# Order of the three-term products: high part of the weights for all k first, then the low part

## Chip, cores and metric

One core of a Trainium2 chip runs the whole program in one launch. The metric is the device time in microseconds (us), as the median of several runs. Before the change it is 2635.63 us (three runs, 2633.51 to 2636.17).

## The reference, cut to what matters

Two token groups, 128 context tokens and 512 latent tokens, pass through two layers with the same weights. Each layer is feed-forward, mixer, feed-forward, each with a modulated norm ahead of it and a gated residual behind it:

```
hn = modulate(rms_norm(x, norm_g[i, 0]), m[:, 0], m[:, 1])
x  = x + 0.5 * m[:, 2] * swiglu(hn, w_gate, w_up, w_down)     # 1024 -> 2816 -> 1024
hn = modulate(rms_norm(x, norm_g[i, 1]), m[:, 3], m[:, 4])
x  = x + m[:, 5] * mix(hn)        # layer 0: SSD scan + pooling; layer 1: gMLP + convolution
hn = modulate(rms_norm(x, norm_g[i, 2]), m[:, 6], m[:, 7])
x  = x + 0.5 * m[:, 8] * swiglu(hn, ...)
```

`swiglu(h) = (silu(h @ w_gate) * (h @ w_up)) @ w_down`. Everything is float32.

## The kernel before

**Tiling.** Activations lie transposed: channels on the 128 partitions, all 640 tokens in the free dimension, cut into two halves A and B of 320. A product with 1024 input channels is a sum over k = 0..7 of 128x128 weight blocks against 128x320 activations; the down projections of the feed-forward sum over the 5 or 6 hidden blocks of a group.

**Three terms.** To keep float32 accuracy with the fast F32R matmul, weights and activations are each split into a high part (a cast) and a low part (source minus high): ScalarE writes `wh`, then VectorE writes `wl` (`w_split`, L219 and L220); activations likewise (`split`, L376 and L377; `apply_mod`, L385 and L387). A block is then three matmuls in one PSUM bank, high x high, high x low, low x high (`mm3`, L392, L393, L394). The weights of one output block, for all k, are a *unit*: one `wh` and one `wl` tile, so each is written by one instruction, 128x1024 for eight blocks and 128x768 for six.

**Units.** `run_units` (L396) makes input projections, a unit at a time, k by k; with `kouter` it goes over k outside and over the units inside. In layer 0's mixer the first unit of half B is `dt`, 32 columns wide (L1016). `out_mms` (L425) makes output projections, through `out_task` (L430, one half) or `out_add` (L438, both halves, where `late=1` holds the last k back in the first block). The pooling branch of that mixer (`pool_mm`, L906) has an output projection of four k. The last output projection of a feed-forward or mixer goes through `out_phase` with `last`: its tasks come in the order A0 A1 A2 A3 B0 A4 B1 A5 B2 A6 B3 A7 B4 B5 B6 B7, so that a unit stays in use over three more A tasks. After B4 stands the matmul of the next norm's sum (`finish`, L368), and the next stage begins in `boundary` with half A, k outside, while half B is still being normed.

**Buffers.** All `wh` and `wl` tiles share a ring of nine buffers (`WB`, L30), four and a half units; raw weights have four (`RB`). A `wl` that finds no free buffer waits until TensorE has read the tile that lies there for the last time.

**Feed-forward.** Gate and up of most hidden blocks are made in `products` (L748) with seven instead of eight products per pair of halves (P1 to P7, sums of weights and of activations); a product is four k blocks x three terms = twelve matmuls (L761 to L764). A PSUM bank takes several products in turn, and ScalarE copies it out in between (`tap`, L745), so the next product in a bank waits for the tap. Each of the four feed-forwards has four groups of hidden blocks; a group's products are followed by its down projection.

**Order.** TensorE's order is the program's own. The order of ScalarE, VectorE, GpSimd and SyncE is set when the program is built, by a planner that goes by program order, by when operands are ready in its own timing, and by offsets such as `TAP_EARLY`; each engine then runs its list in that order. Semaphores make an instruction wait for its operands and buffers.

Of the kernel before, what the change touches and what calls it, by code (L numbers as in the profile page):

```python
# [20 lines left out]
TH = 320  # L21
# [38 lines left out]
A, B = 0, 1  # L60
SL = (slice(0, TH), slice(TH, T))
# [12 lines left out]
def build(tc, ap):  # L74
    nc = tc.nc
    V, S, TE, G = nc.vector, nc.scalar, nc.tensor, nc.gpsimd
    ctx = ExitStack()
    with ctx:
# [12 lines left out]
        def nm(p):  # L91
            uid[0] += 1
            return f"{p}_{uid[0]}"
# [35 lines left out]
        def open_phase(bufs):  # L129
            state["ctx"] = ExitStack()  # L130
            state["pool"] = state["ctx"].enter_context(tc.tile_pool(name=nm("phase"), bufs=bufs, reuse_waits="tile"))
# [11 lines left out]
        def psum(cols=512):  # L143
            return pspool.tile([P, cols], F32, tag="ps", name=nm("ps"))
# [17 lines left out]
        units = {}  # L162
# [106 lines left out]
        def W(key):  # L269
            i, left = index[key], LOOK  # L270
            prefetch(i)
            while i + 1 < len(plan) and left > 0:
                i += 1
                left -= 2 if plan[i][0] == "s" else 1
                if wpos[0] <= i and plan[i][0] == "s" and not state.get("sums"):
                    break
                prefetch(i)
            return loaded[key]
# [3 lines left out]
        def open_mod():  # L282
            crow[:] = [state["pool"].tile([P, D], F32, tag=f"crow{i}", name=nm("crow"), bufs=1) for i in range(2)]
            junk[:] = [state["pool"].tile([P, D], mybir.dt.bfloat16, tag="junk", name=nm("junk"), bufs=1)]
            for i, t in enumerate(crow):
                if kept:
                    nc.scalar.dma_start(out=t, in_=kept[0][i].partition_broadcast(P))
                else:
                    nc.scalar.dma_start(out=t, in_=ap["cc"][i].partition_broadcast(P))
                    S.activation(out=t, in_=t, func=AF.Silu)  # L290
            if not kept:
                kept.append(dpool.tile([2, D], F32, name="silu_rows"))
                for i, t in enumerate(crow):
                    nc.scalar.dma_start(out=kept[0][i:i + 1], in_=t[0:1, :])
            mod_load()
# [79 lines left out]
        def split(src, hi, lo):  # L375
            S.copy(hi, src)  # L376
            V.tensor_sub(lo, src, hi)  # L377
# [13 lines left out]
        def mm3(ps, wh, wl, xh, xl, start, stop):  # L391
            TE.matmul(ps, lhsT=wh, rhs=xh, start=start, stop=False)  # L392
            TE.matmul(ps, lhsT=wh, rhs=xl, start=False, stop=False)  # L393
            TE.matmul(ps, lhsT=wl, rhs=xh, start=False, stop=stop)  # L394

        def run_units(H, keys, hn, kouter=False, mid=None):  # L396
            pss = []
            ws = []
            for key in keys:
                ws.append(W(key))  # L400
                pss.append(psum())

            def one(i, k):
                wh, wl = ws[i]
                m = units[keys[i]][2]
                mm3(pss[i][:m, :TH], wh[k], wl[k], hn.hi(k, H), hn.lo(k, H), k == 0, k == 7)
            if kouter:
                for k in range(8):
                    for i in range(len(keys)):
                        one(i, k)  # L410
                    if mid and k in mid:
                        mid[k]()
            else:
                for i in range(len(keys)):
                    for k in range(8):
                        one(i, k)
            return pss

        def x_update(H, m, ps, L, gidx):
# [3 lines left out]
                                       in1=x[m][:, a:b], op0=ALU.mult, op1=ALU.add)  # L423

        def out_mms(H, ps, w, sh, sl, ks, n):  # L425
            wh, wl = w
            for k in ks:
                mm3(ps[:, :TH], wh[k], wl[k], sh[k][:, SL[H]], sl[k][:, SL[H]], k == 0, k == n - 1)

        def out_task(H, m, key, sh, sl, L, gidx, last):  # L430
            n = len(sh)
# [238 lines left out]
        def ffn(L, f, prev):  # L670
            isc, ish, ig = (1, 0, 2) if f == 0 else (7, 6, 8)
            head = HEAD.get((L, f), NSTD)
            keys = [[("g", L, f, j), ("u", L, f, j)] for j in range(head)]
# [3 lines left out]
            def h_tile(j):  # L677
                hts[j] = state["pool"].tile([P, 2, T], F32R, tag="h", name=nm("h"), bufs=6)

            def post(H, j, pg, pu):  # L680
                if j not in hts:
                    h_tile(j)
                sg = tmp()
                state["silu"] = S.activation(out=sg, in_=pg[:, :TH], func=AF.Silu).ins
                V.tensor_mul(sg, sg, pu[:, :TH])
                split(sg, hts[j][:, 0, SL[H]], hts[j][:, 1, SL[H]])

            if prev is None:
                hn, pss = startup(keys[0] + keys[1][:1])
                open_phase(1)  # L690
                open_mod()
                for H in (A, B):
                    post(H, 0, pss[H][0], pss[H][1])
                for H in (A, B):
                    pu, = run_units(H, keys[1][1:], hn)
                    post(H, 1, pss[H][2], pu)
            else:
                hn, pa = boundary(keys[0] + keys[1], L, isc, ish, prev, Quads)
                open_phase(1)
                post(A, 0, pa[0], pa[1])  # L700
                post(A, 1, pa[2], pa[3])
                for j in range(2):
                    pb = run_units(B, keys[j], hn)
                    post(B, j, pb[0], pb[1])
                with tc.issue_after(state["silu"]):
                    open_mod()
# [36 lines left out]
            def tap(src):  # L743
                t = tmp()
                S.copy(t, src[:, :TH])  # L745
                return t

            def products(js, lead=()):  # L748
                bank, got, ended = {}, {}, set()
                for j, p in product_order(js, lead):  # L750
                    if p == "P1":
                        W(("s", L, f, j))
                    wh, wl = loaded["s", L, f, j][p]
                    xh, xl = X[p]
                    b = "a" if p in CHAIN[0] else "c" if p in CHAIN[1] else "b"
                    if (j, b) not in bank:
                        bank[j, b] = psum()
                    ps = bank[j, b]
                    first = p in ("P1", "P5", "P2")
                    final = p in ("P4", "P3", "P2")  # L760
                    for k in range(4):  # L761
                        for n, (l, r) in enumerate(((wh, xh), (wh, xl), (wl, xh))):
                            TE.matmul(ps[:, :TH], lhsT=l[k], rhs=r[:, k, :], start=(first and k == 0 and n == 0),  # L763
                                      stop=(k == 3 and n == 2), skip_group_check=True)  # L764
                    with tc.high_priority(offset=TAP_EARLY):
                        if p in ("P1", "P6", "P7", "P5"):
                            got[j, p] = tap(ps)
                        if p == "P2":
                            V.tensor_add(got[j, "P1"], ps[:, :TH], got[j, "P1"])
                            S.activation(out=got[j, "P1"], in_=got[j, "P1"], func=AF.Silu)  # L770
                        if p == "P3":
                            V.tensor_add(got[j, "P6"], ps[:, :TH], got[j, "P6"])
                            S.activation(out=got[j, "P6"], in_=got[j, "P6"], func=AF.Silu)
                        if (p == "P7" and (j, "P5") in got) or (p == "P5" and (j, "P7") in got):
                            V.tensor_add(got[j, "P7"], got[j, "P7"], got[j, "P5"])
                        ended.add((j, p))
                        if p in ("P4", "P3") and (j, "P4") in ended and (j, "P3") in ended:
                            hf = ph.tile([P, T], F32, tag="hf", name=nm("hf"), bufs=2)
                            V.scalar_tensor_tensor(out=hf[:, SL[A]], in0=bank[j, "a"][:, :TH], scalar=-1.0, in1=got[j, "P1"],
                                                   op0=ALU.mult, op1=ALU.mult)  # L780
                            V.scalar_tensor_tensor(out=hf[:, SL[B]], in0=got[j, "P7"], scalar=-1.0,
                                                   in1=got[j, "P6"], op0=ALU.mult, op1=ALU.mult)
                            h_tile(j)
                            split(hf, hts[j][:, 0, :], hts[j][:, 1, :])
                    if p == "P1":
                        pump(rate_j)
# [793 lines left out]
```

## Time and profile before

| what | value |
|---|---|
| median of the runs | 2635.63 us |
| profiled execution: its own time, its span | 2630.1 us, 2628.3 us |
| granted TensorE clock, mean over the span | 0.991 |
| TensorE matmul | 2520.9 us busy, 96%, 17241 instructions |
| VectorE | 1932.4 us busy, 74% |
| ScalarE | 1226.9 us busy, 47% |
| chain that ended last | 36% TensorE in the shares by engine |

Busy TensorE time counts a matmul until its modelled end, so matmuls that follow each other overlap in the rows: a 128x320 matmul is shown with 0.31 us, and the next starts 0.147 us after it. What TensorE loses shows as a longer step from one start to the next.

### The profile page before, as it was taken

How to read it: one execution, taken by the hardware profiler on the slowest of the kernel's cores; microseconds unless marked ns; L12 is line 12 of the kernel's file. 1: busy time of each engine (PE TensorE's matmuls, PEld its weight loads, DVE VectorE, ACT ScalarE, POOL GpSimd, SP SyncE). 2: the span in 40 equal slices, each digit the busy share in tenths (PEclk: the TensorE clock that was granted, in tenths of full speed). 3: DMA queues.
4: the chain of work that ended last, by engine and by line, in shares of the span. 5: the costliest groups of instructions: out<-in, count | busy, mean ns of one | idle time of the engine just before them, and what ended most of it. 6: DMA issues, size and time to landing. Idle time of an engine off the chain costs nothing. (4 is left out here: it accounts for less than half of the span.)

```text
span 2628.3 us, 43699 instructions
## 1 busy us (share of the span) xinstructions
PE 2520.9 (96%) x17241; PEld 2431.4 (93%) x17241; DVE 1932.4 (74%) x3259; ACT 1226.9 (47%) x2299; POOL 153.6 (6%) x254
## 2 busy tenths in 40 slices
PE   7999999999999999999999999999999999999997
PEld 5999989899989999999899999989879999999997
DVE  6878878689986977777687778766885749554465
ACT  4443535458763535445454444433223525444552
POOL 0011010000000010110001011000000000101100
PEclk9999999999999999999999999999999999999999
DMA  7487785122122476776337687634432124656641
GB/s 285 135 214 211 209 223 170 58 71 66 55 62 78 119 212 176 214 211 164 109 103 218 182 219 222 167 101 128 130 107 71 51 73 132 176 134 154 155 120 59
DMA packets 139650, 377.31 MB, mean 144 GB/s; under 512 B 17458, under 2 KB 24114, under 8 KB 138932
## 3 DMA queue, kind: packets, MB, share of 16 engines
q1 hardware_dynamic: 111280, 296.06, 34.4%
q0 software_dynamic: 24624, 70.79, 15.4%
q10 hardware_dynamic: 3540, 7.66, 0.9%
q8 instruction: 135, 2.21, 0.3%
q14 instruction: 71, 0.58, 0.1%
HBM read 328.39 MB, written 3.68 MB: 126 GB/s over the span
## 5 line engine op out<-in xcount | busy, mean ns | idle before, releaser
L220 DVE TENSOR_TENSOR wl<-wr,wh 128x1024 fp32r<-128x1024 f32 (+3 forms) x393 | 390.9, 998 | 282.0 <-ACT wh L219 109.2
L219 ACT CAST wh<-wr 128x1024 fp32r<-128x1024 f32 (+3 forms) x393 | 339.7, 869 | 398.7 <-DMA wr<-in_wd 134.9
L394 PE MATMUL ps<-h,wl 128*128 128x320 f32 x1408 | 437.9, 311 | 9.8 <-DVE wl L220 9.8
L392 PE MATMUL ps<-h,wh 128*128 128x320 f32 x1408 | 437.6, 311 | 4.3 <-ACT h L376 4.3
L393 PE MATMUL ps<-h,wh 128*128 128x320 f32 x1408 | 437.1, 310 | 1.5 <-DVE h L377 1.5
L763 PE MATMUL ps<-quad,wh 128*128 128x320 f32 x1800 | 400.4, 310 | 5.4 <-ACT tmp L745 5.0
L763 PE MATMUL ps<-th,wh 128*128 128x320 f32 x1200 | 377.0, 314 | 26.0 <-ACT tmp L745 21.5
L763 PE MATMUL ps<-th,wl 128*128 128x320 f32 x1200 | 374.8, 312 | 3.2 <-DVE wl L220 3.2
L763 PE MATMUL ps<-tl,wh 128*128 128x320 f32 x1200 | 374.4, 312 | 0.0
L323 DVE CUSTOM_DVE_ANT_0 junk<-wm,crow,cv 128x1024 bf16<-128x1024 f32 x256 | 327.7, 1280 | 3.0
L392 PE MATMUL ps<-pair,wh 128*128 128x320 f32 (+1 forms) x976 | 308.9, 317 | 5.7 <-ACT pair L385 1.5
L763 PEld LDWEIGHTS ps<-quad,wh 128*128 128x128 f32 x1800 | 302.3, 189 | 6.5 <-ACT tmp L745 5.8
L393 PE MATMUL ps<-pair,wh 128*128 128x320 f32 (+1 forms) x976 | 304.1, 312 | 1.6 <-DVE pair L387 1.4
L394 PE MATMUL ps<-pair,wl 128*128 128x320 f32 (+1 forms) x976 | 303.3, 311 | 0.0
L763 PE MATMUL ps<-quad,wl 128*128 128x320 f32 x900 | 279.2, 310 | 0.7 <-DVE wl L220 0.7
L394 PEld LDWEIGHTS ps<-h,wl 128*128 128x128 f32 x1408 | 265.2, 188 | 14.0 <-DVE wl L220 14.0
L392 PEld LDWEIGHTS ps<-h,wh 128*128 128x128 f32 x1408 | 265.4, 188 | 5.4 <-ACT h L376 5.1
L393 PEld LDWEIGHTS ps<-h,wh 128*128 128x128 f32 x1408 | 265.3, 188 | 3.1 <-DVE h L377 2.4
L763 PEld LDWEIGHTS ps<-th,wh 128*128 128x128 f32 x1200 | 228.1, 190 | 32.1 <-ACT tmp L745 26.8
L220 DVE TENSOR_TENSOR wl<-ws,wh 128x1024 fp32r<-128x1024 f32 x150 | 182.9, 1221 | 97.6 <-ACT wh L219 42.2
L763 PEld LDWEIGHTS ps<-th,wl 128*128 128x128 f32 x1200 | 228.3, 190 | 4.6 <-DVE wl L220 4.5
L763 PEld LDWEIGHTS ps<-tl,wh 128*128 128x128 f32 x1200 | 228.4, 190 | 0.0
(261 smaller groups left out, 4416.4 us busy)
## 6 DMA issues: line engine op xcount, KB each, us to landing
wm<-in_wm SPq DMA_DIRECT2D x128, 512.0 KB, 4.4
wr<-in_wgu SPq DMA_DIRECT2D x75, 512.0 KB, 4.4
ws<-in_wgu SPq DMA_DIRECT2D x150, 256.0 KB, 4.0
ws<-in_wgu POOLq DMA_DIRECT2D x75, 512.0 KB, 5.7
x<-y POOLq DMA_DIRECT2D x96, 320.0 KB, 5.6
wr<-in_wd SPq DMA_DIRECT2D x64, 384.0 KB, 3.5
wr<-in_wd SPq DMA_DIRECT2D x64, 320.0 KB, 3.6
wr<-in_wgu SPq DMA_DIRECT2D x75, 256.0 KB, 3.5
```

The source lines that it names most:

```text
L219: S.copy(hi, src)
L220: state["paced"] = V.tensor_sub(lo, src, hi).ins
L323: V.tensor_tensor_reduce(out=junk[0], in0=w, in1=crow[cond], scale=1.0, scalar=cvc("b_mod", L * 72 + idx * KC + c), op0=ALU.mult, op1=ALU.add,
L392: TE.matmul(ps, lhsT=wh, rhs=xh, start=start, stop=False)
L393: TE.matmul(ps, lhsT=wh, rhs=xl, start=False, stop=False)
L394: TE.matmul(ps, lhsT=wl, rhs=xh, start=False, stop=stop)
L763: TE.matmul(ps[:, :TH], lhsT=l[k], rhs=r[:, k, :], start=(first and k == 0 and n == 0), stop=(k == 3 and n == 2), skip_group_check=True)
```

## The change

A helper `mm_high_first` issues, for the given k, high x high and high x low of each k, and only then low x high of each k. `out_mms` always uses it. `run_units` uses it where k is inside, except for the first `paced` units of a call; only the call for half B after a feed-forward's boundary passes 1 there (for its first pair of units), and all others leave it at 0. The `kouter` path keeps `mm3`. In `products` the loops over k and over the three terms change places: four high x high, four high x low, four low x high. The matmuls are the same in number and shape.

```diff
+        def mm_high_first(ps, w, xh, xl, ks, n):
+            wh, wl = w
+            for k in ks:
+                TE.matmul(ps, lhsT=wh[k], rhs=xh[k], start=(k == 0), stop=False)
+                TE.matmul(ps, lhsT=wh[k], rhs=xl[k], start=False, stop=False)
+            for k in ks:
+                TE.matmul(ps, lhsT=wl[k], rhs=xh[k], start=False, stop=(k == n - 1))
+
-        def run_units(H, keys, hn, kouter=False, mid=None):
+        def run_units(H, keys, hn, kouter=False, mid=None, paced=0):
...
                 for i in range(len(keys)):
-                    for k in range(8):
-                        one(i, k)
+                    if i < paced:
+                        for k in range(8):
+                            one(i, k)
+                    else:
+                        mm_high_first(pss[i][:units[keys[i]][2], :TH], ws[i], [hn.hi(k, H) for k in range(8)],
+                                      [hn.lo(k, H) for k in range(8)], range(8), 8)
...
         def out_mms(H, ps, w, sh, sl, ks, n):
-            wh, wl = w
-            for k in ks:
-                mm3(ps[:, :TH], wh[k], wl[k], sh[k][:, SL[H]], sl[k][:, SL[H]], k == 0, k == n - 1)
+            mm_high_first(ps[:, :TH], w, [t[:, SL[H]] for t in sh], [t[:, SL[H]] for t in sl], ks, n)
...
-                    pb = run_units(B, keys[j], hn)
+                    pb = run_units(B, keys[j], hn, paced=1 - j)
...
-                    for k in range(4):
-                        for n, (l, r) in enumerate(((wh, xh), (wh, xl), (wl, xh))):
+                    for n, (l, r) in enumerate(((wh, xh), (wh, xl), (wl, xh))):
+                        for k in range(4):
                             TE.matmul(ps[:, :TH], lhsT=l[k], rhs=r[:, k, :], start=(first and k == 0 and n == 0),
                                       stop=(k == 3 and n == 2), skip_group_check=True)
```

## Rows read from the trace of the kernel before

**Rows 1.** Part 1 of the page: busy us (share of span) x instructions, by engine.
```profile
PE 2520.9 (96%) x17241; PEld 2431.4 (93%) x17241; DVE 1932.4 (74%) x3259; ACT 1226.9 (47%) x2299; POOL 153.6 (6%) x254
```

**Rows 2.** TensorE's waits, whole span: waiter, releaser, total us, times, longest us.
```profile
PE ps L763 <- ACT tmp L745: 26.5, 23, 4.0
PE ps L394 <- DVE wl L220: 16.8, 24, 0.9
...
PE ps L763 <- DVE wl L220: 3.9, 6, 0.7
```

**Rows 3.** Timeline of TensorE in the startup: start, us, instruction; first and last of 21.
```profile
36.83 0.60 PE L604 MATMUL ps<-quad,wl 128*128 128x320 f32 x3
...
39.91 0.60 PE L604 MATMUL ps<-quad,wh 128*128 128x320 f32 x3
```

**Rows 4.** Timeline of TensorE within products; first and last of 36 matmuls.
```profile
1000.10 0.31 PE L763 MATMUL ps<-th,wh 128*128 128x320 f32 x1
...
1005.23 0.31 PE L763 MATMUL ps<-th,wl 128*128 128x320 f32 x1
```

**Rows 5.** Timeline of TensorE, last down projection (six k), start of task A7.
```profile
1755.78 0.31 PE L393 MATMUL ps<-h,wh 128*128 128x320 f32 x1
1756.70 0.41 PE L394 MATMUL ps<-h,wl 128*128 128x320 f32 x1 [0.61 <-DVE wl L220]
```

**Rows 6.** Timeline of VectorE, same place; in brackets the idle time before.
```profile
1754.45 0.49 DVE L364 TENSOR_TENSOR tmp<-tmp,tmp 128x320 f32<-128x320 f32 x1 [0.59 <-ACT tmp L360]
1755.68 0.96 DVE L220 TENSOR_TENSOR wl<-wr,wh 128x768 fp32r<-128x768 f32 x1 [0.74 <-PE ps L393]
```

**Rows 7.** Timeline of TensorE, last output projection of layer 0's mixer (eight k).
```profile
817.07 0.31 PE L393 MATMUL ps<-slab,wh 128*128 128x320 f32 x1
818.25 0.41 PE L394 MATMUL ps<-slab,wl 128*128 128x320 f32 x1 [0.88 <-DVE wl L220]
```

**Rows 8.** Timeline of TensorE, first products of a feed-forward.
```profile
2226.93 0.42 PE L763 MATMUL ps<-th,wh 128*128 128x320 f32 x1 [0.87 <-ACT wh L219]
2227.19 0.31 PE L763 MATMUL ps<-tl,wh 128*128 128x320 f32 x1
2228.20 0.41 PE L763 MATMUL ps<-th,wl 128*128 128x320 f32 x1 [0.70 <-DVE wl L220]
```

**Rows 9.** Timeline of TensorE and VectorE, first task of the last down projection.
```profile
2569.07 0.31 PE L392 MATMUL ps<-h,wh 128*128 128x320 f32 x1
...
2570.56 0.82 DVE L377 TENSOR_TENSOR h<-hf,h 128x640 fp32r<-128x640 f32 x1 [0.80 <-ACT h L376]
...
2571.44 0.41 PE L393 MATMUL ps<-h,wh 128*128 128x320 f32 x1
```

**Rows 10.** Timeline of TensorE, last block of the pooling projection's first task.
```profile
769.87 0.63 PE L393 MATMUL ps<-pair,wh 128*128 128x320 f32 x1
770.30 0.47 PE L394 MATMUL ps<-pair,wl 128*128 128x320 f32 x1
770.56 1.27 PE L368 MATMUL ps<-tmp,ones_d 128*128 128x320 f32 x2
```

**Rows 11.** Timeline of TensorE, block 6 of the dt unit, half B: high x low.
```profile
524.06 0.33 PE L393 MATMUL ps<-pair,wh 128*32 128x320 f32 x1 [0.25 <-DVE pair L387]
```

**Rows 12.** Stretches: us; busy us (x) of PE, PEld, DVE, ACT, POOL; clock; DMA.
```profile
1660.00:1665.00 5.00, 3.30 (x12) 3.30 (x13) 2.48 (x4) 2.84 (x5) 0.75 (x1) 0.58 0.71 133
1765.00:1770.00 5.00, 5.00 (x36) 5.00 (x36) 5.00 (x7) 2.82 (x5) 0.85 (x16) 1.00 0.39 147
```

**Rows 13.** Timeline of VectorE and ScalarE: boundary's reciprocal; a cast ahead of taps.
```profile
1764.54 2.16 DVE L371 RECIPROCAL tmp<-tmp 128x320 f32<-128x320 f32 x1
...
1660.28 1.04 ACT L219 CAST wh<-ws 128x1024 fp32r<-128x1024 f32 x1 [7.42 <-DMA ws<-in_wgu]
1661.23 0.74 ACT L745 COPY tmp<-ps 128x320 f32<-128x320 f32 x2
```

## The prediction, made before the changed kernel was run

> **What bounds the kernel now.** Read part 1 of the page first: TensorE is busy 96% of the span, VectorE 74% and ScalarE 47% [rows 1]. So the time is TensorE's stream plus its holes, and a reordering can only gain in the holes or by a shorter step between matmuls. Second, TensorE's waits over the whole span [rows 2]: the largest is for taps, the next for low weights, `wl` in output projections and units, 24 times, and `wl` in products, 6 times. Third, the timeline around one wait of each kind, because the idle time that is shown starts only at the modelled end of a matmul: the true loss is the step from start to start, less the usual step. That step is (1005.23 - 1000.10) / 35 = 0.147 us [rows 4].
>
> **Part 1: the step itself.** The same number of matmuls remains. What differs is the neighbour: before, high x high and high x low of a block share their weights; in products after the change no two neighbours do, which undoes 2100 such pairs (6300 matmuls of L763, a third of them). The startup has a stretch without such pairs, 21 matmuls from 36.83 to 39.91: 0.147 us each [rows 3], the same as with pairs [rows 4]. Reading to 0.01 us over 21 steps bounds the difference at 0.0005 us a matmul, 1 us over 2100 pairs, either way. I take 0. The Trainium skill speaks against it: TensorE: Matmul & The Clock Gate, Part 3, "The mechanism", says that a weight load overlaps matmuls in flight only where the row groups differ, which full 128x128 blocks never do; with its 107 ns per 128 columns (section "LDWEIGHTS", an estimate) a load that a pair had spared would cost 2100 x 0.107 = 224 us. This trace doesn't bear that out: there are as many loads as matmuls, 17241 [rows 1], so no load is spared today. It stays as a rival.
>
> **Part 2: low weights in the last output projections.** 24 waits [rows 2] are four in each of six phases that run A0 A1 A2 A3 B0 A4 B1 A5 and so on: four down projections with six k and two mixers with eight. Nine buffers hold four units and one tile, so the low part of unit 4 needs the buffer of unit 0's high part, and that is read last in B0, just ahead of A4. VectorE shows it: `wl` starts after 0.74 us of idle time that ended with L393, the second last matmul of the B task, and takes 0.96 us [rows 6]. TensorE meanwhile has done two matmuls of the next A task and waits: 1756.70 - 1755.78 - 0.15 = 0.77 us [rows 5], and with eight k 818.25 - 817.07 - 0.15 = 1.03 us [rows 7]. Sum: 16 x 0.77 + 8 x 1.03 = 20.6 us.
>
> In the new order the high part is read last by matmul 12 of 18 instead of 17 (16 of 24 instead of 23), 0.74 or 1.03 us earlier, and the low part is wanted at matmul 13 instead of 3 (17 instead of 3), 1.47 or 2.06 us later. Together 2.2 or 3.1 us, against holes of 0.77 or 1.03. VectorE can use the earlier release: what stands ahead of `wl` in its list ended at 1754.94, 0.74 us before `wl` began [rows 6]. Late next would be the high part of unit 5, which waits for the low part of unit 0, free at the end of B0 as before, and is wanted only after A4 and B1: 36 matmuls, 5.3 us. I take the whole 20.6 us; the ends are 0 (the price if another wait stands behind) and 20.6.
>
> **Part 3: low weights in products.** After a late cast, `wl` follows the cast by its own time: 2228.20 - 2227.19 - 0.15 = 0.86 us lost [rows 8]. Six waits with 3.9 us of idle time [rows 2], each 0.16 short of the step (0.86 against 0.70), make 4.9 us. Now eight matmuls with high weights come first, 8 x 0.147 = 1.18 us, and more with the slow first step; the third matmul stands 1.27 us behind the first [rows 8]. So the hole closes but for 0.1 us. Part of the gain is lost again: most of these places are followed by a wait for a tap, which ends when ScalarE has finished its casts, not when TensorE arrives. Bounds 0 and 4.9; I take the middle, 2.4.
>
> **Part 4: activations that are just in time.** The last k is now wanted at two thirds of a task instead of its end, and all low terms still stand behind it. (a) The first task of each feed-forward's last down projection: the low part of the last hidden block is ready at 2570.56 + 0.82 = 2571.38, and its matmul starts at 2571.44 in a task that began at 2569.07 [rows 9]. The new order comes there at 2569.07 + 11 x 0.147 = 2570.69, waits to the same 2571.44, and has six low terms left instead of one: 5 x 0.147 = 0.74, four times, 2.9 us. (b) The pooling projection's first task ends with block 3 arriving at 769.87, and steps are 0.26 there [rows 10]; three more low terms behind it: 0.8 us. (c) In the dt unit the last late arrival is block 6 at 524.06 [rows 11]; ten matmuls stand behind it instead of four: 0.9 us. Together 4.6; bounds 0 (each swallowed by a later wait) and 4.6. I take 4.6. Where the down projection of an earlier group holds its last k back, that part has one k and its order is the same. The first pair of units after a boundary keeps one unit in the old order, and half B has arrived by the second: nothing.
>
> **Part 5: high weights freed earlier in products.** The last read moves from matmul 11 of 12 to 8, 3 x 0.147 = 0.44 us. Casts and low parts that wait for a buffer could start that much sooner, and some of the 26.5 us behind taps [rows 2] could go. All 23 waits shortened by 0.44 would be 10 us. Some carry a slow stretch behind them: after the wait for a transferred tile at 1660 the granted clock of 1660 to 1665 is 0.58 [rows 12]. Bounds 0 and 10 us; I take 0, since most of these casts wait for a transfer [rows 13], not for a buffer.
>
> **Sum.** -20.6 - 2.4 + 4.6 = -18.4 us against the profiled execution's 2630.1 us: 2611.7. The median of the runs, 2635.63, is 5.5 above that execution, so 2617 us, 0.7% less.
>
> **Rivals.**
> Boundary takes it back (15%). VectorE is busy 5.00 of 5 us when half A is normed for the next stage [rows 12]; if its backlog, not TensorE, sets when the next stage runs, half of the 20.6 returns there: 2627 us. Against: the backlog begins with the reciprocal at 1764.54 [rows 13], which waits for TensorE's own matmul behind B4 and moves with it.
> Earlier buffers help (13%): part 5 at its far end, 2607 us. For: VectorE's 74%. Against: the transfers.
> Low weights stay late (7%): `wl` is held by something else in VectorE's list, for instance because the planner puts it behind a later update. Then parts 2 and 4 leave 2635.6 + 4.6 - 2.4 = 2638 us, no change that can be told. Against: VectorE idles before nearly every instruction there [rows 6].
> Slower through taps (7%): the planner orders ScalarE anew by its own timing, and a tap lands behind a cast that waits for a transfer, as at 1660.28, where the cast followed 7.42 us of idle time and the tap came after it [rows 13]. If the 26.5 us double, 2617 + 26.5 = 2644 us; from 18.4 us more on the change is a loss. For: 23 places; against: the list's order and the offset for taps are unchanged.
> Pairs were cheaper (2%): a pair spares something that the change takes away. The bound of part 1 speaks against it. The page's rule named there would be a cause of this kind. It decides from 18.4 / 2100 = 0.009 us a pair; a whole load, 2431.4 / 17241 = 0.141 us [rows 1], would make 296 us, a time of 2913.
>
> **Chances.** My sum has 56%, with a range of its own of 2611 to 2624 (part 3 at either end, part 4 absorbed, part 5 at half). A measurement of this kernel tells about 0.2%, 5.3 us, from no change. Faster by more: 56 + 13 + 15 = 84%. Within it: 7%. Slower: 9%. The range of 8 in 10 takes in both faster rivals: 2605 to 2630.
>
> **What would show it.** Right: no wait of TensorE for `wl` in the six last projections, so a period of 36 or 48 matmuls, 5.3 and 7.1 us, for A4 to A7; `wl` on VectorE released by TensorE two thirds into a B task; holes of about 0.75 us longer in each first task of a last down projection. Wrong: a step other than 0.147 us in products; new waits of TensorE at the boundaries behind these projections; more than 26.5 us behind taps, or fewer.

## The result, and the profile after

The changed kernel takes 2604.99 us (median of four runs, 2602.65 to 2608.83); the kernel before took 2634.57 beside it (four runs, 2630.33 to 2636.17). The ratio is 0.9893, with a 95% interval of 0.9876 to 0.9909: about 28 us less. Forecast were 2617 us, 18.4 us less, and a range of 2605 to 2630. The direction was right. The time stands at the very end of the range, 12 us below the forecast, so it is partly luck that the range holds, and the sizes have to be explained. The profiled executions stand at 2630.1 and 2602.65 us, 27.5 apart.

Part 1 of the page after the change: busy us (share of span) x instructions. Against [rows 1], as many matmuls and weight loads, and the same work within 4 us on each engine; only the span is shorter. Almost all that was won was idle time of TensorE.

```profile
PE 2517.2 (97%) x17241; PEld 2429.7 (93%) x17241; DVE 1931.5 (74%) x3259; ACT 1227.8 (47%) x2301; POOL 154.0 (6%) x254
```

TensorE's waits over the whole span after the change (waiter, releaser, total us, times, longest us). Both rows for `wl` of [rows 2] are gone from the list, 16.8 and 3.9 us. Taps did not grow (21.9 against 26.5), but they have not shrunk for certain either: in a second profile of the changed kernel, taken with the experiments, they take 28.0 us (the third fence). Two rows grew: the high and the low part of `h`, which the first tasks of last down projections wait for; the second fence has them in the kernel before.

```profile
PE ps L774 <- ACT tmp L756: 21.9, 26, 2.3
...
PE ps L400 <- ACT h L376: 6.1, 5, 1.9
...
PE ps L401 <- DVE h L377: 3.4, 7, 0.8
```

```profile
PE ps L392 <- ACT h L376: 4.3, 3, 1.9
...
PE ps L393 <- DVE h L377: 1.5, 4, 0.4
```

```profile
PE ps L774 <- ACT tmp L756: 28.0, 25, 4.6
```

TensorE in the last down projection with six k, where [rows 5] showed the hole (start, us, instruction). A task is now 12 matmuls with high weights (L400, L401) and 6 with low ones (L403). From the first start of a task to its first low one 1731.79 - 1730.03 = 1.76 us = 12 x 0.147; to the next task 1732.66 - 1731.79 = 0.87 = 6 x 0.145. No step is longer than the usual one.

```profile
1730.03 0.31 PE L400 MATMUL ps<-h,wh 128*128 128x320 f32 x1
...
1731.64 0.31 PE L401 MATMUL ps<-h,wh 128*128 128x320 f32 x1
1731.79 1.04 PE L403 MATMUL ps<-h,wl 128*128 128x320 f32 x6
1732.66 0.31 PE L400 MATMUL ps<-h,wh 128*128 128x320 f32 x1
...
1734.42 1.04 PE L403 MATMUL ps<-h,wl 128*128 128x320 f32 x6
```

VectorE at the same place, answering to [rows 6]: `wl` has no bracket, so VectorE did not stand idle for it. Its buffer comes free when VectorE comes to it: the last matmul with high weights of the B task, number 12 of 18, ends at 1731.64 + 0.31 = 1731.95, VectorE's instruction before ends at 1731.50 + 0.49 = 1731.99, and `wl` starts at 1731.98. It is 5.28 us behind the `wl` before it, 36 matmuls of 0.147, and done at 1732.94, 1.48 us before the first low term of the next A task (1734.42).

```profile
1726.70 0.96 DVE L220 TENSOR_TENSOR wl<-wr,wh 128x768 fp32r<-128x768 f32 x1
...
1731.50 0.49 DVE L364 TENSOR_TENSOR tmp<-tmp,tmp 128x320 f32<-128x320 f32 x1 [0.60 <-ACT tmp L360]
1731.98 0.96 DVE L220 TENSOR_TENSOR wl<-wr,wh 128x768 fp32r<-128x768 f32 x1
```

TensorE in products (four matmuls of one kind to a row). The first two rows are 28 matmuls apart: (2202.83 - 2198.73) / 28 = 0.146 us, with no two neighbours sharing weights, as in [rows 4] with them. The other three are the first products after a late cast, as in [rows 8]: the low terms begin 2205.72 - 2204.45 = 1.27 us behind the first matmul, that is 8 x 0.147 and one slow step of 0.10 more. The hole of 0.86 is closed.

```profile
2198.73 0.75 PE L774 MATMUL ps<-quad,wh 128*128 128x320 f32 x4
...
2202.83 0.75 PE L774 MATMUL ps<-th,wl 128*128 128x320 f32 x4
2204.45 0.85 PE L774 MATMUL ps<-th,wh 128*128 128x320 f32 x4 [0.87 <-ACT wh L219]
2205.14 0.74 PE L774 MATMUL ps<-tl,wh 128*128 128x320 f32 x4
2205.72 0.85 PE L774 MATMUL ps<-th,wl 128*128 128x320 f32 x4
```

**Where the 27.7 us of span came from.** All steps of TensorE from start to start over 0.2 us, less 0.147 each, summed by what ended the wait, before and after: low weights in units and output projections 21.0 and 0.3; slow steps that have no wait of their own 88.6 and 86.4 (the step behind each hole is slow, and so are steps at the lower clock); low weights in products 4.9 and 0; taps 30.2 and 26.3; operands at boundaries and norms (`quad`, `tmp`, `sq`) 15.7 and 10.8. Against that `h` 7.3 and 12.1, and `pair` 8.7 and 12.4. All of them: 192.2 and 163.9, 28.3 less. The second profiles of both kernels (2630.6 and 2606.5 us of span) agree for low weights, 21.0 to 0.4 and 4.9 to 0, and for the losses, `h` 7.2 to 10.3 and `pair` 9.1 to 12.4. They do not for the rest: taps 33.2 to 32.6, boundaries and norms 14.6 to 12.2, all 194.4 to 170.0, 24.4 less. So two executions of one kernel differ by up to 6 us in taps alone.

**Where it lost.** First, in the first task of a last down projection. These rows are ScalarE, VectorE and TensorE of one of the four. A weight cast that waited 2.11 us for its transfer stands ahead of the cast of `h`; the high part comes late, then the low part, and only then can the low terms run (454.82), six of them, that filled this time in the old order. The order of the two casts is new: the second fence has ScalarE at this place in the kernel before, with `h` first. The planner changed it, and by the profiles it did so where products release their high weights earlier (all runs below in which the release is at matmul 8 or 9), not where only output projections are changed.

```profile
452.20 0.83 ACT L219 CAST wh<-wr 128x768 fp32r<-128x768 f32 x1 [2.11 <-DMA wr<-in_wd]
452.94 0.72 ACT L376 CAST h<-hf 128x640 fp32r<-128x640 f32 x1
...
453.69 0.83 DVE L377 TENSOR_TENSOR h<-hf,h 128x640 fp32r<-128x640 f32 x1 [1.63 <-ACT h L376]
...
453.71 0.42 PE L400 MATMUL ps<-h,wh 128*128 128x320 f32 x1 [0.82 <-ACT h L376]
454.57 0.41 PE L401 MATMUL ps<-h,wh 128*128 128x320 f32 x1 [0.44 <-DVE h L377]
454.82 1.04 PE L403 MATMUL ps<-h,wl 128*128 128x320 f32 x6
```

```profile
456.24 0.73 ACT L376 CAST h<-hf 128x640 fp32r<-128x640 f32 x1 [1.90 <-DVE hf L779]
457.62 0.84 ACT L219 CAST wh<-wr 128x768 fp32r<-128x768 f32 x1 [0.65 <-DMA wr<-in_wd]
```

Second, the dt unit. Stretches of us; busy us (x instructions) of PE, PEld, DVE, ACT, POOL; granted clock; DMA share; GB/s. First the kernel after, then the kernel before at the same place. While half B's activations arrive one by one TensorE does fewer matmuls after (16 in 6 us against 23), because the eight low terms wait for the end; and in the 5 us that follow the granted clock is 0.50, the 1.2 GHz level, with 21 matmuls where the next 5 us hold 36. Before, the clock stayed at 1.00. The 15 matmuls missing are 15 x 0.147 = 2.2 us. The clock fell at this place in all three profiles with the new order here (0.66 over 5 us in the second profile of the changed kernel and in that of units alone) and in none of the ten with the old order, but also in that of the last run below, which has the old order here. So the order of the dt unit is not the whole cause.

```profile
512.00:518.00 6.00, 3.88 (x16) 1.18 (x14) 5.83 (x13) 4.18 (x13) 0.75 (x11) 0.85 0.00 1
518.00:523.00 5.00, 5.00 (x21) 4.11 (x20) 1.29 (x2) 1.36 (x2) 0.00 (x0) 0.50 0.28 105
523.00:528.00 5.00, 5.00 (x36) 4.77 (x36) 3.38 (x7) 2.37 (x3) 0.00 (x0) 1.00 0.29 93
```

```profile
518.00:524.00 6.00, 4.11 (x23) 1.76 (x21) 5.72 (x13) 4.59 (x14) 0.74 (x11) 1.00 0.00 0
524.00:530.00 6.00, 5.94 (x41) 5.45 (x42) 3.23 (x6) 2.74 (x4) 0.00 (x0) 1.00 0.24 89
```

### The profile page after: what moved, and what is told of

Same layout as the page of the kernel before. It is cut to its first block, busy times and chain, and to the rows that moved or that the text cites. A ratio compares the mean times of both kernels' runs of the same rounds, so it can differ in the third digit from the quotient of the medians.

```text
span 2600.6 us, 43735 instructions
## 1 busy us (share of the span) xinstructions
PE 2517.2 (97%) x17241; PEld 2429.7 (93%) x17241; DVE 1931.5 (74%) x3259; ACT 1227.8 (47%) x2301; POOL 154.0 (6%) x254
## 5 line engine op out<-in xcount | busy, mean ns | idle before, releaser
L400 PE MATMUL ps<-h,wh 128*128 128x320 f32 x1408 | 420.9, 311 | 6.1 <-ACT h L376 6.1
L401 PE MATMUL ps<-h,wh 128*128 128x320 f32 x1408 | 420.2, 311 | 3.4 <-DVE h L377 3.4
L774 PE MATMUL ps<-quad,wh 128*128 128x320 f32 x1800 | 300.9, 309 | 2.1 <-ACT tmp L756 2.1
L400 PEld LDWEIGHTS ps<-h,wh 128*128 128x128 f32 x1408 | 265.9, 189 | 7.9 <-ACT h L376 7.4
L400 PE MATMUL ps<-pair,wh 128*128 128x320 f32 (+1 forms) x880 | 268.1, 318 | 5.0 <-ACT pair L376 2.2
L401 PEld LDWEIGHTS ps<-h,wh 128*128 128x128 f32 x1408 | 265.8, 189 | 5.4 <-DVE h L377 5.0
L401 PE MATMUL ps<-pair,wh 128*128 128x320 f32 (+1 forms) x880 | 264.1, 313 | 1.8 <-DVE pair L377 0.9
L403 PE MATMUL ps<-h,wl 128*128 128x320 f32 x1408 | 252.6, 309 | 0.0
L774 PE MATMUL ps<-th,wh 128*128 128x320 f32 x1200 | 228.9, 313 | 24.3 <-ACT tmp L756 19.8
L774 PE MATMUL ps<-th,wl 128*128 128x320 f32 x1200 | 225.8, 310 | 0.0
L774 PE MATMUL ps<-tl,wh 128*128 128x320 f32 x1200 | 225.7, 310 | 0.0
L403 PEld LDWEIGHTS ps<-h,wl 128*128 128x128 f32 x1408 | 218.6, 188 | 0.0
L774 PEld LDWEIGHTS ps<-th,wh 128*128 128x128 f32 x1200 | 188.0, 189 | 31.8 <-ACT tmp L756 26.1
L774 PEld LDWEIGHTS ps<-th,wl 128*128 128x128 f32 x1200 | 189.0, 189 | 0.4
L219 ACT CAST wh<-ws 128x1024 fp32r<-128x1024 f32 x150 | 157.2, 1050 | 67.2 <-DVE ws L245 39.0
L756 ACT COPY tmp<-ps 128x320 f32<-128x320 f32 x300 | 125.8, 424 | 120.1 <-PE ps L774 118.4
```

Of the source, the lines that this page charges most:

```text
L400: TE.matmul(ps, lhsT=wh[k], rhs=xh[k], start=(k == 0), stop=False)
L401: TE.matmul(ps, lhsT=wh[k], rhs=xl[k], start=False, stop=False)
L403: TE.matmul(ps, lhsT=wl[k], rhs=xh[k], start=False, stop=(k == n - 1))
```

## The experiments

The theory: low weights are wanted later, so the holes of [rows 5, 7, 8] close, and activations that arrive last cost some of it back. The rival: high weights are read for the last time earlier, so buffers come free earlier, and that gives the gain, in output projections, in products or in both. Ratios are against the kernel before, run in turns on the same chip. How fine they are is shown by one of the runs below: the kernel before against itself came to 0.9984 (0.9966 to 1.0002), so under about 0.2% nothing is told apart.

**Output projections alone.** Only `out_mms` has the new order.

```diff
-            for k in ks:
-                mm3(ps[:, :TH], wh[k], wl[k], sh[k][:, SL[H]], sl[k][:, SL[H]], k == 0, k == n - 1)
+            if high_first: mm_high_first(TE, ps[:, :TH], w, [t[:, SL[H]] for t in sh], [t[:, SL[H]] for t in sl], ks, n)
```

> Only the output projections take the new order; input units and products keep the old one. Theory (low weights of the last output projections wait for a buffer): the 24 waits for wl go, each 0.87 us (six k) or 1.15 us (eight k) with the slow first step behind it, 16 x 0.87 + 8 x 1.15 = 23 us less; against it some 3 to 6 us for activations that are just in time (first tasks of the last projections, pooling, convolution): 17 to 20 us less than before, and the six waits for wl in products stay. Rival (the gain comes from products, where high weights come free earlier and the taps wait less): under 8 us less.

Measured 2616.41 against 2637.68: 0.9923 (0.9905 to 0.9942), 20 us less. In its trace the waits for `wl` in projections are gone, those in products stay (3.2 us, 5 times). Most of the gain is here.

**Products alone.**

```diff
-                    for k in range(4):
-                        for n, (l, r) in enumerate(((wh, xh), (wh, xl), (wl, xh))):
+                    for n, (l, r) in enumerate(((wh, xh), (wh, xl), (wl, xh))):
+                        for k in range(4):
```

> Only the products take the new order. Theory: the six waits for wl in products go, 5 us less, and the waits behind taps change by no more than 4 us either way; the 24 waits of the last output projections stay. In all 1 to 9 us less. Rival (products carry the gain): 15 us less or more.

Measured 2622.63 against 2637.68: 0.9948 (0.9935 to 0.9961), 14 us less. The holes of low weights in products are worth 4.9 at most, so something else gains here, and the theory does not have it. It also speaks against the rival by which sharing weights with the neighbour spared time. Run once more, later, with the next ones:

> The products alone in the new order again, on the same chip as the run above. It measured 0.9948 [0.9935, 0.9961]. If that holds: 0.993 to 0.9965. If it was a chance of the runs (its profile shows only 4 us less): 0.997 to 0.999.

0.9958 (0.9941 to 0.9976), 11 us: the gain is real.

**Units alone.** `run_units` has the new order, with `paced` as in the change; projections and products do not.

```diff
-                    for k in range(8):
-                        one(i, k)
+                    for k in range(8 if i < paced else 0): one(i, k)
+                    if i >= paced: mm_high_first(TE, pss[i][:units[keys[i]][2], :TH], ws[i], [hn.hi(k, H) for k in range(8)], [hn.lo(k, H) for k in range(8)], range(8), 8)
...
-                    pb = run_units(B, keys[j], hn)
+                    pb = run_units(B, keys[j], hn, paced=1 - j)
```

> Only the input units take the new order. Theory: nothing to gain, since no unit waits for wl in the kernel before, but the dt unit ends about 1 us later by its eight low terms: 0 to 3 us more. Rival (hidden waits in the units): 3 us less or more.

Measured 2640.19 against 2637.68: 1.0014 (1.0000 to 1.0028). Nothing is gained in units; the loss of 2 to 4 us agrees with the dt unit but is too small to be told from none.

**Only the A tasks of the six last projections.** This keeps when high weights of a unit are released (that is in its B task) and takes only the later need.

```diff
-            out_mms(H, ps, w, sh, sl, range(n), n)
+            out_mms(H, ps, w, sh, sl, range(n), n, last and H == A)
```

> Only the A tasks of the six last output projections take the new order, so wl is wanted 10 or 14 matmuls later, but the high part is freed as late as before (it is read last in the B tasks, which keep the old order). Theory: later need alone closes the holes, 23 us less, and the first A tasks of four down projections lose 0.74 us each: 20 us less. Rival (the earlier release of the high part is what closes them): the holes stay, 0 to 3 us more than before.

Measured 2617.19 against 2637.68: 0.9921 (0.9903 to 0.9938), 21 us less. VectorE still waits for the second last matmul of B tasks, with the same total that this stretch had before; in the list of TensorE's waits there, which follows in the second fence, `wl` stands no more. The later need alone closes these holes.

```profile
DVE wl L220 <- PE ps L393: 3.6, 5, 0.7
```

```profile
PE ps L1585 <- ACT h L376: 2.0, 1, 2.0
PE ps L1586 <- DVE h L377: 0.5, 1, 0.5
PE ps L368 <- DVE tmp L364: 0.4, 1, 0.4
PE ps L392 <- ACT pair L385: 0.3, 1, 0.3
PE ps L393 <- DVE pair L387: 0.3, 1, 0.3
```

**Only the B tasks of the six last projections.** The other side: earlier release, and need as before.

```diff
-            out_mms(H, ps, w, sh, sl, range(n), n)
+            out_mms(H, ps, w, sh, sl, range(n), n, last and H == B)
```

> Only the B tasks of the six last output projections take the new order: the high part is freed 5 or 7 matmuls earlier (0.74 or 1.03 us), and wl is wanted as early as before. Theory (either side of the slack is enough): holes of 0.77 and 1.03 us shrink to under 0.1, 20 to 23 us less, with no loss in first A tasks. Rival (only the later need counts): the 24 waits stay, within 3 us of before.

Measured 2612.78 against 2638.28: 0.9917 (0.9893 to 0.9942), 22 us less. Here too TensorE's waits for `wl` outside products are gone. Either side alone is enough, as 0.74 us of earlier release or 1.47 of later need against a hole of 0.77 would have it; in the change both act, and the second adds nothing that these runs can tell. At the boundaries the two differ: waits for `quad` take 7.1 us from start to start here, 7.1 to 7.5 in all profiles whose B tasks have the new order, and 9.4 to 9.9 in all others, that of the A tasks alone (9.5) among them. So some 2.4 us at boundaries come with the new order of the B tasks; by what way was not looked into.

**Products: later need without earlier release.** The last high x low term goes to the end: `wl` is wanted at matmul 8 (9 in the change), and the high part is free only after matmul 12, one later than in the kernel before.

```diff
+                    for i, (l, r, k) in enumerate([(wh, xh, k) for k in range(4)] + [(wh, xl, k) for k in range(3)]
+                                                  + [(wl, xh, k) for k in range(4)] + [(wh, xl, 3)]):
```

> Only products are changed, in another order: four high x high, three high x low, four low x high, and the last high x low at the end. wl is wanted at matmul 8 instead of 3, but the high part is read last by the last matmul, so it comes free no earlier than before, and the planner's order of ScalarE is nearly that of the kernel before. Products in the new order alone measured 0.9948 of before. Theory (later need alone): waits for wl in products go, ratio 0.995 to 0.998. Rival (earlier release of high parts, or the planner's other order that goes with it, makes more than half of the 0.9948): ratio 0.998 to 1.000.

Measured 2638.66 against 2638.28: 1.0003 (0.9987 to 1.0019). From start to start its waits for `wl` in products fell from 4.9 to 0.8 us; taps take 29.8 us, against 26.5 and 29.1 in two profiles of the kernel before. So the closed holes of [rows 8] gain nothing here that can be measured: this speaks against the theory in products.

**Products: one matmul moved.** The same, but that last high x low term stands ninth, so that the high part is free after matmul 9.

```diff
+                    seq = [(wh, xh, k) for k in range(4)] + [(wh, xl, k) for k in range(3)] + [(wl, xh, k) for k in range(4)]
+                    for i, (l, r, k) in enumerate(seq[:8] + [(wh, xl, 3)] + seq[8:]):
```

> Products alone: four high x high, three high x low, one low x high, the last high x low, three low x high. wl is wanted by matmul 8, one sooner than the last high term, and the high part comes free at matmul 9, one later than in the new order (8) and three sooner than in the run with late release (12, ratio 1.0003). If the release decides: between 0.995 and 0.998. If the exact order of the new kernel is needed: 0.999 to 1.001.

Measured 2622.34 against 2638.27: 0.9952 (0.9934 to 0.9971), 13 us less, as much as the order of the change. Against the run before, one matmul moved, and with it the release of the high part, makes the difference.

**Products: earlier release without later need.** High part free after matmul 9, `wl` wanted at matmul 3.

```diff
+                    hh, hl, lh = ([(l, r, k) for k in range(4)] for l, r in ((wh, xh), (wh, xl), (wl, xh)))
+                    for i, (l, r, k) in enumerate([hh[0], hl[0], lh[0], hh[1], hl[1], hh[2], hl[2], hh[3], hl[3]] + lh[1:]):
```

> Products alone, the complement of the run with late release: wl is wanted by matmul 3 as before, but the high part is read last by matmul 9 of 12 instead of 11, so it comes free 0.29 us earlier. If the earlier release (with the planner's order that follows from it) makes the gain of products: ratio 0.995 to 0.998 of before, with the six waits for wl still there. If only the two together make it, or the later need alone: 0.999 to 1.001.

Measured 2631.65 against 2638.27: 0.9978 (0.9961 to 0.9994), 6 us less, hardly more than the kernel against itself shows. The holes stay (`wl` 3.9 us, 7 times). Late need alone 0, early release alone some 6, both 11 to 14.

VectorE's rows for `wl` over the whole span, those that change with products, show that the release acts on its list: idle time that nothing shown ended ("issue"), that a product's matmul ended, that a tap ended. In order: kernel before; high part free at 12; free at 9. The order that gains nothing leaves these as they were. With the release at 9 the first two shrink by 40 us, but 24 of them return behind taps: VectorE stands elsewhere in its list, it is not idle much less. Early release alone shows nearly the same (42.1, 53.4 and 25.9), so these rows do not explain why it gains less.

```profile
DVE wl L220 <- issue: 67.4, 33, 5.6
DVE wl L220 <- PE ps L763: 61.5, 32, 5.0
...
DVE wl L220 <- ACT tmp L745: 0.9, 1, 0.9
```

```profile
DVE wl L220 <- issue: 73.4, 35, 5.2
DVE wl L220 <- PE ps L763: 58.9, 32, 4.3
```

```profile
DVE wl L220 <- PE ps L763: 47.8, 30, 3.8
DVE wl L220 <- issue: 40.7, 16, 5.2
DVE wl L220 <- ACT tmp L745: 24.2, 16, 3.1
```

What is not separated: the planner, which goes by when buffers come free, gives VectorE and ScalarE another order when the release moves (products alone against before: 315 of VectorE's 3259 places and 141 of ScalarE's 2299 hold another instruction in the profiles; with the release at 9 it is 186 and 94, with the release at 12 only 20 and 2). Earlier buffers and the new order of these engines came together in each of these runs. A tenth buffer, which would have shown the buffers alone, was not tried.

**The kernel before, profiled again.** In the profiles, products alone gain only 2630.1 - 2626.5 = 3.6 us, the medians 11 to 15. Perhaps the usual executions of the kernel before wait more for taps than the profiled one.

> The kernel before again, for a second profile of it. The first profiled execution took 2630.1 us, while its median on the chips of the experiments is 2638. If the products' gain beyond the waits for wl lies in waits behind taps that the first profile had few of, this one shows a longer time with the difference in those waits: 5 to 10 us more than the 30 us lost there in the first. If it also takes about 2630 with about 30 us, the gain stays without a place.

The second profile stands at 2632.36 us (median of its eight executions 2633.15), with 29.1 us behind taps, 25 times, and the same waits for `wl` (16.8 and 3.6): this idea is not borne out. What does differ is the granted clock. These rows are span and mean granted clock, first of this profile, then of products with the release at 9:

```profile
core 0: 2630.6 us, clock 0.991
```

```profile
core 0: 2621.0 us, clock 0.994
```

Summed over stretches of 5 us, (1 - granted clock) x 5 is 25.6 and 25.8 us in the two profiles of the kernel before, 24.4 with the release at 12 and 17.4 with the release at 9. So the clock makes some 8 of the 9.5 us by which the two executions shown differ (2632.36 and 2622.82). The clock falls to its lower level at 6 to 14 scattered places of a profiled execution, behind stretches with holes, and not at the same ones in each. Each run lists its mean clock, so the executions can be set against each other; 0.001 of the mean clock is 0.001 x 2630 = 2.6 us of full speed, an estimate (twelve executions with the release at 12 go from 2630.2 us at 0.992 to 2646.6 at 0.987, 3.3 us for 0.001; over all 160 executions of the experiments, each against the mean of its kernel, it is 2.6). Means over all executions, differences to the kernel before on the same chip:

| kernel | executions | mean clock (before) | difference, us | by the clock | the rest |
|---|---|---|---|---|---|
| output projections alone | 6 | 0.9885 (0.9898) | -20.6 | +3.3 | -23.9 |
| products alone | 5 | 0.9914 (0.9898) | -13.7 | -4.3 | -9.4 |
| products alone, again | 11 | 0.9914 (0.9897) | -11.0 | -4.3 | -6.6 |
| products, release at 9 | 6 | 0.9928 (0.9897) | -14.3 | -8.2 | -6.1 |
| products, early release alone | 12 | 0.9921 (0.9897) | -7.0 | -6.2 | -0.8 |
| products, later need alone | 12 | 0.9896 (0.9899) | +0.9 | +0.9 | -0.1 |
| units alone | 12 | 0.9888 (0.9898) | +3.3 | +2.7 | +0.6 |
| the kernel before, again | 8 | 0.9910 (0.9899) | -5.0 | -2.9 | -2.1 |

The last row is the kernel before against itself, so 2 to 3 us of either part tell nothing. With this in mind the gain in products seems to have two parts: 4 to 8 us that go with a higher clock, in the rows with an earlier release and not in that with the later need alone; and 6 to 9 us that come only where the release is earlier and the need later, and in which the closed holes of 4.9 are contained. The two profiles of products alone show these holes closed and no more: all slow steps, counted as above, add up to 188.7 and 189.0 us, against 192.2 and 194.4 in the two of the kernel before, and taps take 32.2 and 30.6 of them, against 30.2 and 33.2. What took back the closed holes where the release is at 12 stays open: its taps, 33.9, are no longer than the second profile of the kernel before has them. That the clock is the cause and not a sign of fewer holes was not tried by itself.

**The change without its losses.** The whole change, but the dt unit of half B and the first A task of each projection through `out_task` keep the old order.

```diff
-            out_mms(H, ps, w, sh, sl, range(n), n)
+            out_mms(H, ps, w, sh, sl, range(n), n, not (H == A and m == 0))
...
-            ps, = run_units(B, first[:1], hn)
+            ps, = run_units(B, first[:1], hn, paced=1)
```

> The whole change, but the tasks whose activations come just in time keep the old order: the dt unit of half B, and the first A task of every output projection that goes through one-half tasks (last projections, pooling, convolution). Theory: what the change lost there comes back, 2.9 us in the dt unit (0.9 for its low terms and 2 for the half clock behind it), about 4 in four first tasks of the down projections, 0.8 in pooling, 1.8 in the convolution's first task: 5 to 10 us less than the changed kernel on the same chip, 33 to 40 less than before. The granted clock after the dt unit stays at full. Rival (the arrivals are late anyway and the next wait swallows it): within 3 us of the changed kernel.

> The changed kernel again, for comparison on the same chip: ratio 0.988 to 0.991 of before.

Measured 2600.08 against 2638.28: 0.9864 (0.9837 to 0.9892); the change on the same chip 2611.43, 0.9901 (0.9877 to 0.9925). That is some 10 us for the better, though the intervals overlap. By the medians this version beats both kernels. Its mean clock over six executions is 0.9922, that of the change beside it 0.9895: by the estimate above 7 of the 10 us. The change itself has no higher clock than the kernel before (0.9899), though products alone have; perhaps its late low terms cost what its products gained there, but no run shows it. In the profile all waits for `h` together are 3.9 us, the largest of them shown below; they were 9.5 and 7.7 in the two profiles of the changed kernel and 5.8 before. The full clock behind the dt unit that was expected did not come: the clock dips to 0.75 over 5 us, with 28 matmuls, where the changed kernel had 0.50 and 21 in one profile and 0.66 in the other.

```profile
PE ps L1585 <- ACT h L376: 1.9, 1, 1.9
```

```profile
513.00:520.00 7.00, 5.19 (x29) 2.62 (x28) 6.63 (x15) 5.15 (x15) 0.75 (x11) 0.93 0.00 1
520.00:525.00 5.00, 5.00 (x28) 4.71 (x27) 2.02 (x3) 1.36 (x2) 0.00 (x0) 0.75 0.34 94
```

## Why the prediction was right, and where its sizes were wrong

**Part 1 (0) held.** The step in products is 0.146 us without shared neighbours, and products alone are faster, not slower. The rival that pairs were cheaper fell, and with it what the page cited there would have made of the time.

**Part 2 (-20.6) held in mechanism and nearly in size.** Matching the matmuls of both traces by number, each closed hole gives back 0.87 us with six k and 1.15 with eight: 16 x 0.87 + 8 x 1.15 = 23.1. The forecast took the hole up to the late matmul and left out that the next step behind any wait is slow too, 0.25 instead of 0.147. In the change the buffer's release does come two thirds into the B task, as forecast. The gain is kept through the boundaries: the lead in the matched starts does not fall behind any of them (the loss in the dt unit, which follows the first, is counted in part 4), so the rival that the boundary takes it back fell. So did the one that low weights stay late.

**Part 3 (-2.4) took half where the whole came.** The holes of 4.9 us are closed in the change and in products alone, and the slow steps of products alone fall by about as much. The reason that the forecast gave for taking half, that taps take some of it back, is not borne out: taps are as long as before within what two executions differ by. In the order with the release at 12 the closed holes gained nothing (1.0003), and no run shows what took them back.

**Part 4 (+4.6) was right in kind and too small.** By matched starts: 1.68, 1.79 and 0.73 us lost in three first tasks of last down projections and 0.45 won in the fourth, which had waited for a transfer in the old order too (forecast 2.9, together 3.75); the pooling projection 0.8, as forecast; the dt unit 3.3 instead of 0.9, through the clock; the convolution's projection 1.8, not foreseen. Together 9.6. The loss of 0.73 is the forecast's 0.74; in the two tasks that lost more, the missed point was ScalarE's new list, in which a weight cast that waits for its transfer stands ahead of the cast of `h`.

**Part 5 (0) is the term with the weakest ground.** "I take 0, since most of these casts wait for a transfer [rows 13], not for a buffer." With the release after matmul 8 or 9 products gain 11 to 14 us, with the release after 12 nothing; for products alone the bound of 10 us was nearer than the value taken. One cast that waits for a transfer [rows 13] stood for all. ScalarE's waits in the kernel before bear out "most": 249.5 us before 105 casts of weights for transfers. But the row below stands beside them, casts that wait until products have read a buffer, and VectorE's `wl` waits 61.5 us in 32 places for the same.

```profile
ACT wh L219 <- PE ps L763: 33.8, 30, 1.3
```

The way that the forecast named, shorter waits behind taps, is not what the profiles show: taps take 27.9 and 26.7 us in the two of products alone and 21.9 and 28.0 in the two of the change, against 26.5 and 29.1 before. The forecast had noted that some waits carry a stretch of low clock behind them [rows 12], and then left it out of the sum; in products alone a higher clock goes with 4 to 8 of the 11 to 14 us, in the whole change with none. So the rival "earlier buffers help", given 13%, was right that the release decides in products, and its mechanism is not shown. The rival that taps double fell by the same numbers.

**The sum again**, from the first two profiles: -23.1 for part 2, -4.9 for part 3, +8.5 for part 4 (`h` 4.8, `pair` 3.7) make -19.5, close to the forecast's -18.4, because a part 4 that is too small and parts 2 and 3 that are too small cancel. That is luck. The other 9 us are what the forecast had at nothing: 3.9 less behind taps, and 4.9 less at boundaries and norms; from the second two profiles 0.6 and 2.4. Only the 2.4 at boundaries, which come with the B tasks, are shown to be the change's; the rest is no more than executions of one kernel differ by.

## What to carry to other kernels

Where operands of a sum come at different times and share a ring of buffers, two lists decide the order of the terms: which operand is late (put it last), and which is wanted back by the producer (read it out first); ask the producer's own waits for a buffer, not only the consumer's holes. Where the other operand arrives just in time, as in the first task behind a producer, an order that fills the holes with terms already there looks better, by the one run that tried it (some 10 us, with overlapping intervals). An earlier release can also make a planner reorder other engines, as it did with the casts of `h`. And of two remedies for one hole, expect the gain once.

## What the runs showed of the hardware that was not expected

After a stretch in which TensorE had many holes of under a microsecond (16 matmuls in 6 us, clock 0.85), it ran for 5 us at half speed (0.50) although it was busy throughout. The number of matmuls ahead does not tell by itself: at the same place the kernel before had 23 in 6 us and kept 1.00, and units alone had 24 and fell to 0.66. Such falls come at 6 to 14 places of a profiled execution and not always at the same ones. The mean clocks are 0.987 to 0.994 for the kernel before, with some 2.6 us for each 0.001; over all executions of the experiments the mean clock goes with a little over half of the variance between executions of one kernel (57%). Where medians and profiles of two kernels disagree, the mean clock of each execution is the first thing to look at.

The first step behind a wait takes 0.25 or 0.26 us instead of 0.147 where a row shows one (454.82 - 454.57 above, 2227.19 - 2226.93 in [rows 8]), so a closed hole gave 0.1 us more than its length: 0.87 against 0.77.
